# Down projections fed with operand sums from DRAM, in a two-layer decoder trunk on one core

## The chip, the core and the metric

The kernel runs on one core of a Trainium2 chip. Its engines work side by side, each through its own list of instructions: PE (TensorE, matrix products), DVE (VectorE), ACT (ScalarE), POOL (GpSimd) and SP (SyncE, which here issues the DMA transfers). They wait for each other through semaphores. The metric is the device time of one execution in microseconds (us); smaller is better. The clock of PE has two levels, 1.2 and 2.4 GHz; the profile gives the granted clock as a share of the higher one.

## The reference

The program is a decoder trunk of two layers over one sequence of 1024 tokens with 1024 features, all in float32. Each layer is a token mixer (HGRN2 in layer 0, a Griffin recurrent block in layer 1) and a SwiGLU feed-forward block of 2816 hidden features, each behind an RMSNorm and with a residual add. Only the feed-forward blocks and the residual stream are touched here:

```python
def swiglu(h, w_in, w_out):
    gate, up = jnp.split(h @ w_in, [D_FF], axis=-1)
    return (jax.nn.silu(gate) * up) @ w_out

for l in range(DEPTH):
    hn = rmsnorm(x, norm_mix[l])
    mix = hgrn2_mixer(hn, ...) if l % N_MIXERS == 0 else rglru_mixer(hn, ...)
    x = x + mix
    x = x + swiglu(rmsnorm(x, norm_ffn[l]), ffn_w_in[l], ffn_w_out[l])
return rmsnorm(x, norm_final)
```

## The kernel before

**Number format.** Every float32 operand of a large product is split in two float32r tiles, hi and lo: ACT copies the value into hi (`act(hi[:], src, AF.Copy)`), and DVE or POOL subtracts (lo = value − hi). A product of two such operands is three matmuls, hi·hi, hi·lo and lo·hi, recorded at L263, L264 and L265. Tiles are 128 partitions by 512 elements ([P, H]); instructions issued through a helper that records their order all carry line 93.

**Gate and up.** The feed-forward input product runs over 22 tiles f of 128 hidden features. Each tile takes seven quarter products (Winograd's form of Strassen's algorithm), 84 matmuls in all. The weight quarters a11, a12, a21, a22 (tiles `raw_fi`) come from DRAM; `sums` (L983 to L986) makes the left-hand factors s1 to s4 on POOL; ACT and DVE split them. The products gather in PSUM banks pa, pb, pc, pd; DVE and ACT turn these into the two halves of the hidden tile (c11 and u2 or c22), and `store` (L990) writes them to DRAM (`hd`). The tensor engine's order is the program's order.

**Down.** The output product uses the same seven products again, now over 11 pairs j of hidden tiles. It runs in four rounds r over the 11 pairs (`seq`, 44 steps). In rounds 0, 1 and 2 a step feeds two accumulators, pa and pb, of four PSUM banks each, with 24 matmuls; in round 3 only pa, with 12. So a layer has 3×11×24 + 11×12 = 924 matmuls here. At the end of a round `close_a` and `close_b` add the banks to the residual stream `xT` on DVE (`add_x`), before the next round may overwrite them.

**Operands of down, before.** `loads` (L1078 and on) brings parts of `w_out` (`raw_a`) and halves of the hidden tiles (`ht`) from DRAM: 4, 5, 4 and 1 transfers of 256 KB per step in rounds 0 to 3. `items` (L1091 to L1115) makes the factors from them. In round 1 that is two adds on POOL (L1102, L1103; tiles `ds`), three adds on DVE (`ht`, `dt`) and four lo parts on DVE; in round 2 three adds on POOL (L1111 to L1113), one add and four lo parts on DVE; in round 0 two lo parts on DVE and two on POOL; in round 3 one each. `ahead(n + 1, 1)` at each step makes the factors of the next step and issues the loads of the one after it.

**Residual stream, before.** `xT` is 8 tiles of 128 features by 1024 tokens that stay in SBUF for the whole program (L149).

**What sets the order.** Instructions issued through `ordered` or `keep` run in program order on their engine; the others (the adds of `sums`, `store`, the splits on POOL) are placed by the scheduler of the framework. Buffers are handed out by tag (`BUFS`): a tile of a tag waits until an earlier tile of the tag has been read for the last time.

Of the kernel before, what the change touches and what calls it, by code (L numbers as in the profile page):

```python
# [47 lines left out]
def tile_trunk(  # L48
# [56 lines left out]
    BUFS = {"slab": 57, "raw": 6, "whi": 6, "wlo": 6, "F": 1}  # L105
# [80 lines left out]
    def split(name, src, tag="slab", lo_engine=None, kept=False):  # L186
        """src, [P, H] in float32, as the sum of two float32r tiles."""
# [8 lines left out]
    def halves(name, src, lo_engine=None):  # L196
        """As split, with the low part left to a later call; in program order."""
# [13 lines left out]
    def w_cols(name, w, c0, tag="w", lo_engine=None):  # L211
        """Weights of 128 output features: per k-tile (hi, lo)."""
# [8 lines left out]
    def w_row(name, w, r, lo_engine=None, tag="w"):  # L221
        """Weights of 128 input features: per output tile (hi, lo)."""
# [7 lines left out]
    # The tensor engine's order is the program's. Its stream of large products drives side jobs, generators  # L230
    # that yield how much of the stream to let pass before their next step.
# [64 lines left out]
    def row_scale(name, rs, n_bc):  # L296
        """The rows' factors rs, tokens on partitions, along the free axis of all partitions."""
# [1097 lines left out]
```

## Time and profile before

| what | value |
|---|---|
| time, three runs | 2388.19, 2383.64, 2386.39 us (median 2386.39) |
| profiled execution: its span | 2383.3 us, 3.1 us under that median |
| PE busy | 2265.4 us, 95% of the span |
| DVE busy | 1545.5 us, 65% |
| ACT busy | 915.7 us, 38% |
| POOL busy | 833.9 us, 35% |
| transfers, mean | 83 GB/s |

The span is the time from the first to the last record of the profiled execution; nothing else is known of that execution's own time, so sums are made against the span. The stages follow one another: HGRN2 to about 650 us, the first feed-forward block to about 1337 us (its down projection starts at 1098 us), the recurrent block to about 1690 us, and the second feed-forward block (its down projection starts at 2129 us). Shares of the whole span are means over stages with different limits, so each stage has to be read by itself.

### The profile page before, as it was taken

What the parts mean: (1) busy time and instruction counts of PE and PEld (TensorE: products, weight loads), DVE (VectorE), ACT (ScalarE), POOL (GpSimd) and SP (SyncE); (2) the same over time, 40 slices, a digit from 0 to 9 for tenths busy, and PEclk for the clock granted to TensorE, in tenths of its full rate; (3) what the DMA queues carried; (4) which work ended last, traced back from release to release, by engine and by line L of the source; (5) the groups of instructions that cost most, each with busy time, mean ns of one, the idle gap of its engine ahead of it and who ended that gap; (6) DMA issues with size and microseconds to landing.
All of it is one profiled execution on the core that took longest, in us unless ns stands there. A gap on an engine that the chain in (4) does not pass through costs nothing. (4 is left out here: it accounts for less than half of the span.)

```text
span 2383.3 us, 30347 instructions
## 1 busy us (share of the span) xinstructions
PE 2265.4 (95%) x11022; PEld 1892.7 (79%) x11022; DVE 1545.5 (65%) x2578; ACT 915.7 (38%) x1527; POOL 833.9 (35%) x594
## 2 busy tenths in 40 slices
PE   7999999999979999999989899998799999999898
PEld 6898898888758888887768777877678888877777
DVE  6676657647895444445988767668874444448895
ACT  5222121221343333334334465566343333343345
POOL 5102012020353232333576343223543333235672
PEclk9999999999989999999989999999899999999999
DMA  5001101110112222226454211111122222236452
GB/s 143 27 28 45 36 27 41 32 45 19 32 36 89 89 89 84 81 75 228 156 172 137 63 38 55 50 36 36 40 77 88 88 81 84 84 130 224 159 171 93
DMA packets 216568, 197.08 MB, mean 83 GB/s; under 512 B 12009, under 2 KB 159586, under 8 KB 216418
## 3 DMA queue, kind: packets, MB, share of 16 engines
q1 hardware_dynamic: 216418, 195.15, 25.9%
q8 instruction: 86, 1.41, 0.2%
q14 instruction: 64, 0.52, 0.1%
HBM read 167.83 MB, written 27.26 MB: 82 GB/s over the span
## 5 line engine op out<-in xcount | busy, mean ns | idle before, releaser
L983 POOL TENSOR_TENSOR s<-raw_fi,raw_fi 128x512 f32<-128x512 f32 x44 | 60.4, 1372 | 403.2 <-DMA raw_fi<-in_ffn_w_in_dram 383.1
L93 DVE TENSOR_TENSOR lo_x<-ht,hi_x 128x512 fp32r<-128x512 f32 x132 | 143.0, 1111 | 41.0 <-ACT hi_x L93 25.0
L263 PE MATMUL pa<-hi_x,hi_w 128*128 128x512 f32 (+1 forms) x364 | 146.3, 402 | 23.4 <-ACT hi_x L93 15.7
L93 DVE TENSOR_TENSOR lo_s<-s,hi_s 128x512 fp32r<-128x512 f32 x88 | 66.9, 760 | 147.5 <-ACT hi_s L93 147.5
L93 ACT ACTIVATE hi_a<-raw_fi 128x512 fp32r<-128x512 f32 x132 | 83.3, 632 | 194.5 <-PE pc L264 79.1
L265 PE MATMUL pa<-hi_x,lo_w 128*128 128x512 f32 (+1 forms) x364 | 144.9, 398 | 9.4 <-DVE lo_w L93 9.4
L264 PE MATMUL pa<-lo_x,hi_w 128*128 128x512 f32 (+1 forms) x364 | 144.9, 398 | 3.5 <-DVE lo_x L93 3.5
L264 PE MATMUL pa<-lo_t_n,hi_s 128*128 128x512 f32 x336 | 133.4, 397 | 11.5 <-DVE lo_t_n L201 11.5
L191 POOL TENSOR_TENSOR lo_w<-raw_a,hi_w 128x512 fp32r<-128x512 f32 x66 | 91.4, 1392 | 135.1 <-ACT hi_w L93 126.3
L93 DVE TENSOR_TENSOR lo_a<-raw_fi,hi_a 128x512 fp32r<-128x512 f32 x128 | 90.5, 708 | 68.5 <-ACT hi_a L93 68.4
L265 PE MATMUL pa<-hi_t_n,lo_s 128*128 128x512 f32 x336 | 132.9, 395 | 0.0
L263 PE MATMUL pa<-hi_t_n,hi_s 128*128 128x512 f32 x336 | 132.4, 394 | 0.0
L93 ACT ACTIVATE hi_s<-s 128x512 fp32r<-128x512 f32 x88 | 55.6, 632 | 152.1 <-PE pa L264 85.4
L263 PE MATMUL pb<-hi_x,hi_w 128*128 128x512 f32 x264 | 105.0, 398 | 3.8 <-DVE xT L93 3.8
L263 PEld LDWEIGHTS pa<-hi_x,hi_w 128*128 128x128 f32 x364 | 71.7, 197 | 41.6 <-ACT hi_x L93 17.7
L265 PE MATMUL pb<-hi_x,lo_w 128*128 128x512 f32 x264 | 104.4, 395 | 0.0
L264 PE MATMUL pb<-lo_x,hi_w 128*128 128x512 f32 x264 | 104.3, 395 | 0.0
L459 PEld LDWEIGHTS lv<-qp,k 128*128 128x128 f32 x768 | 98.7, 191 | 6.6 <-PE pg L265 0.5
L93 ACT ACTIVATE hi_s<-raw_fi 128x512 fp32r<-128x512 f32 x88 | 55.4, 632 | 126.1 <-PE pd L264 61.0
L93 DVE TENSOR_TENSOR lo_w<-ds,hi_w 128x512 fp32r<-128x512 f32 x88 | 92.1, 1054 | 10.7 <-ACT hi_w L93 10.5
L93 ACT ACTIVATE hi_w<-ds 128x512 fp32r<-128x512 f32 x88 | 54.9, 626 | 110.4 <-PE pb L264 29.4
L459 PE MATMUL lv<-qp,k 128*128 128x64 f32 x768 | 96.3, 267 | 0.1
(357 smaller groups left out, 7053.2 us busy)
## 6 DMA issues: line engine op xcount, KB each, us to landing
raw_a<-in_ffn_w_out_dram SPq DMA_DIRECT2D x220, 256.0 KB, 3.2
raw_fi<-in_ffn_w_in_dram SPq DMA_DIRECT2D x180, 256.0 KB, 3.0
ht<-hd SPq DMA_DIRECT2D x88, 256.0 KB, 5.3
hd<-c SPq DMA_DIRECT2D x48, 256.0 KB, 2.1
hd<-u SPq DMA_DIRECT2D x40, 256.0 KB, 3.0
xr<-in_x_dram SPq DMA_DIRECT2D x16, 256.0 KB, 5.5
raw_v<-in_hgrn_w_in_dram SPq DMA_DIRECT2D x16, 256.0 KB, 3.0
raw_f<-in_hgrn_w_in_dram SPq DMA_DIRECT2D x16, 256.0 KB, 2.8
```

The lines of the kernel that those rows point to most:

```text
L93: ins = f(*args, **kwargs)
L191: ins = (lo_engine.tensor_tensor if lo_engine else tt)(lo[:], src, hi[:], ALU.subtract)
L263: pe(mm(pt, wh, xh, start=st[0], stop=False, skip_group_check=skip))
L264: pe(mm(pt, wh, xl, start=False, stop=False, skip_group_check=skip))
L265: pe(mm(pt, wl, xh, start=False, stop=st[1], skip_group_check=skip))
L459: mm(lvc(c).rearrange("p (b m) -> p b m", m=m), ct(kt, c), second(ct(qp, c)), start=True, stop=True,)
L983: add(s1, a21, a22, ALU.add)
```

## The change

**Sums made early.** In the gate/up loop POOL now also makes the operand sums of the down projection, once per pair j: `x_sums` (four subtractions of hidden halves: t1, t3, t2, t4) and `w_sums` (four loads of `w_out` parts at L1039, then four adds: s1, s3, s2, s4). Each result, and three of the four hidden halves, is written to DRAM by `spill` (L1009). A layer has 44 + 44 such adds.

**Down loads finished operands.** `loads` brings 4 tiles per step in rounds 0 to 2 and 2 in round 3 (14 per pair in both versions); no sum is left in the down projection. `items` only splits: three lo parts on DVE and one on POOL per step of rounds 0 to 2 (all four on DVE before step 4). The splits are made two steps ahead and loads three (`ahead(n + 2, 3)`); those of steps 0 and 1 stand at the end of the gate/up loop, and their hi and lo tiles of the weights use the tags whi and wlo; later ones use slab.

**Residual stream.** `xT` becomes 16 tiles of [P, H] under a tag x with 16 buffers. After the norm ahead of the feed-forward block has read a tile, `put_away` writes it to DRAM; `bring_back` loads 4, 8 and 4 of them ahead of the loads of steps (0, 6), (1, 6) and (3, 4). In between the tag's buffers hold c11, u2, c22 and the tiles of `w_sums` (`da`). The transfers added per layer are 11 × 11 + 32 = 153 of 256 KB.

The core of the diff (removed comments and the parts that follow from it left out):

```diff
-    BUFS = {"slab": 57, "raw": 6, "whi": 6, "wlo": 6, "F": 1}
+    BUFS = {"slab": 57, "x": 16, "raw": 6, "whi": 6, "wlo": 6, "F": 1}
...
-    xT = [cp.tile([P, S], F32, name=f"xT{d}") for d in range(KT)]
+    xT = {}
+    xd = {(d, half): dp.tile([P, H], F32, name=f"xd{d}_{half}") for half in range(NHALF) for d in range(KT)}
...
+    def put_away(d, half):
+        nc.sync.dma_start(xd[d, half][:], half_of(d, half))
+        del xT[d, half]
+
+    def bring_back(ds, half):
+        for d in ds:
+            keep(nc.sync.dma_start(half_of(d, half), xd[d, half][:]))
...
+        def x_sums(j):
+            b12, b11, b22, b21 = [hidden.pop((f, half))[:] for f in (2 * j, 2 * j + 1) for half in range(2)]
+            add(b11, b12, b11, ALU.subtract)
+            spill(hd["t1"][j], b11)
+            add(b12, b22, b12, ALU.subtract)
+            spill(hd["t3"][j], b12)
+            add(b22, b22, b11, ALU.subtract)
+            spill(hd["t2"][j], b22)
+            add(b21, b21, b22, ALU.subtract)
+            spill(hd["t4"][j], b21)
...
+            add(a22, a21, a22, ALU.add)
+            spill(wd["s1"][j], a22)
...
-            s1, s2 = t2k("D", f"ds1{nm}"), t2k("E", f"ds2{nm}")
-            if r == 1:
-                b11, b21, b12, b22 = ht[top, 1][:], ht[bot, 1][:], ld[3], ld[4]
-                keep(add(s1[:], a21, a22, plus))
-                keep(add(s2[:], s1[:], a11, sub))
-                t2 = t2k("A", f"dt2{nm}")
-                tt(b11, b12, b11, sub)
-                tt(t2[:], b22, b11, sub)
-                tt(b21, b21, t2[:], sub)
-                return pair(f"6{nm}", s2[:], t2[:]), pair(f"5{nm}", s1[:], b11)
...
+            keys = (("s2", "t2"), ("s1", "t1")) if r == 1 else (("s3", "t3"), ("s4", "b22"))
+            return [fetch(f"{k}{nm}", d[k][j][:], t) for ks in keys for k, d, t in zip(ks, (wd, hd), ("raw", "slab"))]
...
+            tag = "w" if r == 0 and j < 2 else "slab"
+            first = pair(f"1{nm}", ld[0], ld[1], None if n < 4 else nc.gpsimd, tag)
+            return first, pair(f"2{nm}", ld[2], ld[3], None, tag) if len(ld) > 2 else None
...
+        backs = {(0, 6): [(0, 1)], (1, 6): [(0, 0), (DG, 0)], (3, 4): [(DG, 1)]}
...
-            ahead(n + 1, 1)
-            for m in (2, 3) if r == 3 else ():
+            ahead(n + 2, 3)
+            if n == 5:
+                sums_due()
+            for m in (3, 4, 5) if r == 3 else ():
```

POOL in the gate/up loop of layer 0, around tiles f = 12 and 13. Before it has four sums per tile (`s1`, `s2`, then the two that overwrite `raw_fi`):

```order
L983 TENSOR_TENSOR s1_0_12_8013<-raw_fi0_12_1_0_8009,raw_fi0_12_1_1_8011 128x512
L984 TENSOR_TENSOR s2_0_12_8014<-s1_0_12_8013,raw_fi0_12_0_0_7968 128x512
L986 TENSOR_TENSOR raw_fi0_12_0_0_7968<-raw_fi0_12_0_0_7968,raw_fi0_12_1_0_8009 128x512
L985 TENSOR_TENSOR raw_fi0_12_0_1_7970<-raw_fi0_12_0_1_7970,s2_0_12_8014 128x512
L983 TENSOR_TENSOR s1_0_13_8160<-raw_fi0_13_1_0_8156,raw_fi0_13_1_1_8158 128x512
L984 TENSOR_TENSOR s2_0_13_8161<-s1_0_13_8160,raw_fi0_13_0_0_8115 128x512
L986 TENSOR_TENSOR raw_fi0_13_0_0_8115<-raw_fi0_13_0_0_8115,raw_fi0_13_1_0_8156 128x512
L985 TENSOR_TENSOR raw_fi0_13_0_1_8117<-raw_fi0_13_0_1_8117,s2_0_13_8161 128x512
```

The sums of one tile are followed by those of the next. The same place of the changed kernel, with `da` the parts of `w_out` and `c11`, `u2` the hidden halves of tiles 10 and 11:

```order
L1000 TENSOR_TENSOR s1_0_12_8298<-raw_fi0_12_1_0_8294,raw_fi0_12_1_1_8296 128x512
L1001 TENSOR_TENSOR s2_0_12_8299<-s1_0_12_8298,raw_fi0_12_0_0_8253 128x512
L1023 TENSOR_TENSOR u2_0_10_8013<-c11_0_10_7935,u2_0_10_8013 128x512
L1003 TENSOR_TENSOR raw_fi0_12_0_0_8253<-raw_fi0_12_0_0_8253,raw_fi0_12_1_0_8294 128x512
L1041 TENSOR_TENSOR da0_6_11_8165<-da0_6_10_8163,da0_6_11_8165 128x512
L1043 TENSOR_TENSOR da0_6_10_8163<-da0_6_00_8159,da0_6_10_8163 128x512
L1045 TENSOR_TENSOR da0_6_00_8159<-da0_6_11_8165,da0_6_00_8159 128x512
L1002 TENSOR_TENSOR raw_fi0_12_0_1_8255<-raw_fi0_12_0_1_8255,s2_0_12_8299 128x512
L1047 TENSOR_TENSOR da0_6_01_8161<-da0_6_01_8161,da0_6_00_8159 128x512
L1025 TENSOR_TENSOR c11_0_10_7935<-c11_0_11_8089,c11_0_10_7935 128x512
L1000 TENSOR_TENSOR s1_0_13_8452<-raw_fi0_13_1_0_8448,raw_fi0_13_1_1_8450 128x512
L1001 TENSOR_TENSOR s2_0_13_8453<-s1_0_13_8452,raw_fi0_13_0_0_8407 128x512
```

Between the sums of tile 12 and those of tile 13 six adds now stand on POOL (t1, four of `w_sums`, t3); two more (t2, t4) follow `s2` of tile 13.

SP's list for the same tiles, before: one weight quarter after another, with the two hidden halves of a tile between them.

```order
L990 DMA hd0_10_6015<-c11_0_10_7673 128x512
L93 DMA raw_fi0_13_0_0_8115<-in_ffn_w_in_dram 128x4x128
L990 DMA hd0_10_6015<-u2_0_10_7743 128x512
L93 DMA raw_fi0_13_0_1_8117<-in_ffn_w_in_dram 128x4x128
L93 DMA raw_fi0_13_1_0_8156<-in_ffn_w_in_dram 128x4x128
L93 DMA raw_fi0_13_1_1_8158<-in_ffn_w_in_dram 128x4x128
L990 DMA hd0_11_6016<-c11_0_11_7820 128x512
L93 DMA raw_fi0_14_0_0_8262<-in_ffn_w_in_dram 128x4x128
```

No transfer in it reads what POOL writes. And the list of the changed kernel (`da` loads, `ht1d`, `hb11d`, `ws1d` to `ws4d` the spills):

```order
L1039 DMA da0_6_00_8159<-in_ffn_w_out_dram 128x512
L1039 DMA da0_6_01_8161<-in_ffn_w_out_dram 128x512
L1039 DMA da0_6_10_8163<-in_ffn_w_out_dram 128x512
L1039 DMA da0_6_11_8165<-in_ffn_w_out_dram 128x512
L1009 DMA ht1d0_5_6075<-u2_0_10_8013 128x512
L93 DMA raw_fi0_13_0_1_8409<-in_ffn_w_in_dram 128x4x128
L93 DMA raw_fi0_13_1_0_8448<-in_ffn_w_in_dram 128x4x128
L1009 DMA ws1d0_6_6120<-da0_6_11_8165 128x512
L1009 DMA ws3d0_6_6142<-da0_6_10_8163 128x512
L1009 DMA ws2d0_6_6131<-da0_6_00_8159 128x512
L1009 DMA ws4d0_6_6153<-da0_6_01_8161 128x512
L93 DMA raw_fi0_13_1_1_8450<-in_ffn_w_in_dram 128x4x128
```

The last weight quarter of tile 13 (`raw_fi0_13_1_1`), which `s1` of tile 13 reads, stands behind the four spills of `w_sums`, and these wait for the adds at L1041 to L1047, which stand on POOL behind `s2` of tile 12.

DVE in round 1 of the down projection of layer 0, before: the factors of step (1, 4), from the first sum on, with one sum of step (1, 5) between them.

```order
L93 TENSOR_TENSOR dt20_1_4_10201<-ht0_9_0_10137,ht0_8_1_9563 128x512
L93 TENSOR_TENSOR ht0_8_0_10135<-ht0_9_0_10137,ht0_8_0_10135 128x512
L93 TENSOR_TENSOR ht0_9_1_9567<-ht0_9_1_9567,dt20_1_4_10201 128x512
L93 TENSOR_TENSOR lo_w60_1_4_10206<-ds20_1_4_10198,hi_w60_1_4_10205 128x512
L93 TENSOR_TENSOR lo_x60_1_4_10210<-dt20_1_4_10201,hi_x60_1_4_10209 128x512
L93 TENSOR_TENSOR ht0_10_1_9611<-ht0_10_0_10193,ht0_10_1_9611 128x512
L93 TENSOR_TENSOR lo_x50_1_4_10218<-ht0_8_1_9563,hi_x50_1_4_10217 128x512
L93 TENSOR_TENSOR lo_w50_1_4_10214<-ds10_1_4_10197,hi_w50_1_4_10213 128x512
```

Three sums and four lo parts make one step. The changed kernel, lo parts of steps (1, 3) to (1, 5), where `ld_` tiles are the operands loaded:

```order
L93 TENSOR_TENSOR lo_x20_1_3_10502<-ld_t10_1_3_10359,hi_x20_1_3_10501 128x512
L93 TENSOR_TENSOR lo_x10_1_4_10558<-ld_t20_1_4_10403,hi_x10_1_4_10557 128x512
L93 TENSOR_TENSOR lo_w20_1_4_10562<-ld_s10_1_4_10405,hi_w20_1_4_10561 128x512
L93 TENSOR_TENSOR lo_x20_1_4_10566<-ld_t10_1_4_10407,hi_x20_1_4_10565 128x512
L93 TENSOR_TENSOR lo_x10_1_5_10606<-ld_t20_1_5_10455,hi_x10_1_5_10605 128x512
L93 TENSOR_TENSOR lo_w20_1_5_10610<-ld_s10_1_5_10457,hi_w20_1_5_10609 128x512
L93 TENSOR_TENSOR lo_x20_1_5_10614<-ld_t10_1_5_10459,hi_x20_1_5_10613 128x512
```

Per step seven instructions have become three, and the sums have left the engine.

## Rows read from the trace of the kernel before

**Rows 1.** Page, part 1: busy time, share of span, instructions
```profile
PE 2265.4 (95%) x11022; PEld 1892.7 (79%) x11022; DVE 1545.5 (65%) x2578; ACT 915.7 (38%) x1527; POOL 833.9 (35%) x594
```

**Rows 2.** Windows: gate/up loop, start and middle of a down projection
```profile
core 0: us, PE busy (x) PEld busy (x) DVE busy (x) ACT busy (x) POOL busy (x), PEclk, DMA share, GB/s
750.00:1000.00 250.00, 250.00 (x1104) 207.01 (x1103) 112.19 (x171) 94.08 (x158) 74.28 (x52) 1.00 0.27 83
1120.00:1130.00 10.00, 10.00 (x46) 8.29 (x45) 5.47 (x5) 4.86 (x9) 4.29 (x5) 1.00 1.04 386
1170.00:1290.00 120.00, 108.03 (x439) 86.88 (x439) 112.03 (x124) 46.39 (x82) 84.49 (x46) 0.93 0.52 169
```

**Rows 3.** Groups by line, PE, first down projection: busy | idle, releasers
```profile
L263 PE MATMUL pa<-hi_x,hi_w 128*128 128x512 f32 x139 | 57.1, 410 | 10.9 <-ACT hi_x L93 7.0 <-ACT hi_w L93 3.9
L264 PE MATMUL pa<-lo_x,hi_w 128*128 128x512 f32 x138 | 56.6, 410 | 1.4 <-DVE lo_x L93 1.4
L265 PE MATMUL pa<-hi_x,lo_w 128*128 128x512 f32 x138 | 56.5, 410 | 4.4 <-DVE lo_w L93 4.4
L263 PE MATMUL pb<-hi_x,hi_w 128*128 128x512 f32 x132 | 52.7, 399 | 1.8 <-DVE xT L93 1.8
```

**Rows 4.** The same view of the second down projection
```profile
L263 PE MATMUL pa<-hi_x,hi_w 128*128 128x512 f32 x139 | 56.6, 407 | 9.7 <-ACT hi_x L93 5.8 <-ACT hi_w L93 3.9
L264 PE MATMUL pa<-lo_x,hi_w 128*128 128x512 f32 x138 | 55.7, 404 | 1.3 <-DVE lo_x L93 1.3
L265 PE MATMUL pa<-hi_x,lo_w 128*128 128x512 f32 x138 | 55.7, 404 | 4.9 <-DVE lo_w L93 4.9
L263 PE MATMUL pb<-hi_x,hi_w 128*128 128x512 f32 x132 | 52.3, 396 | 2.0 <-DVE xT L93 2.0
```

**Rows 5.** Windows of both down projections; columns as in rows 2
```profile
1110.00:1120.00 10.00, 8.65 (x31) 7.06 (x32) 8.31 (x6) 5.41 (x10) 8.17 (x6) 0.83 1.01 369
1160.00:1170.00 10.00, 7.74 (x33) 5.82 (x32) 9.70 (x12) 2.83 (x5) 5.02 (x4) 1.00 0.69 242
1170.00:1180.00 10.00, 8.20 (x29) 6.29 (x29) 10.00 (x16) 2.82 (x5) 3.25 (x4) 0.83 0.65 220
1220.00:1250.00 30.00, 21.82 (x71) 16.93 (x70) 26.30 (x28) 12.33 (x22) 24.43 (x15) 0.77 0.55 169
2200.00:2210.00 10.00, 8.22 (x30) 6.26 (x29) 10.00 (x15) 3.20 (x6) 5.13 (x4) 0.83 0.59 197
2250.00:2280.00 30.00, 22.94 (x78) 18.29 (x79) 26.30 (x29) 13.24 (x24) 24.00 (x14) 0.77 0.54 175
```

**Rows 6.** Groups by line, DVE, first down projection
```profile
L93 DVE TENSOR_TENSOR lo_w<-ds,hi_w 128x512 fp32r<-128x512 f32 x44 | 46.1, 1054 | 5.3 <-ACT hi_w L93 5.2
```

**Rows 7.** Groups by line, POOL, first down projection
```profile
L1102 POOL TENSOR_TENSOR ds<-raw_a,raw_a 128x512 f32<-128x512 f32 x11 | 27.6, 2507 | 26.6 <-DVE lo_w L93 21.8 <-DMA ht<-hd 4.8
```

**Rows 8.** Timeline, DVE beside POOL: start, duration, instruction
```profile
685.50 0.68 DVE L93 TENSOR_TENSOR hs_n<-hs_n,hs_n 128x512 f32<-128x512 f32 x1
686.10 1.75 DVE L93 TENSOR_TENSOR lo_s<-s,hi_s 128x512 fp32r<-128x512 f32 x1
```

**Rows 9.** Timeline of POOL at that place
```profile
685.66 1.64 POOL L983 TENSOR_TENSOR s<-raw_fi,raw_fi 128x512 f32<-128x512 f32 x1 [10.06 <-DVE lo_s L93]
```

**Rows 10.** Groups by line, POOL, gate/up loop
```profile
L984 POOL TENSOR_TENSOR s<-s,raw_fi 128x512 f32<-128x512 f32 x17 | 29.5, 1733 | 1.3
L985 POOL TENSOR_TENSOR raw_fi<-raw_fi,s 128x512 f32<-128x512 f32 x17 | 22.0, 1292 | 20.4 <-DVE lo_a L93 20.4
```

**Rows 11.** Timeline, DVE, end of a gate/up tile
```profile
864.97 0.69 DVE L93 TENSOR_TENSOR lo_s<-s,hi_s 128x512 fp32r<-128x512 f32 x1 [2.01 <-ACT hi_s L93]
865.58 0.68 DVE L93 TENSOR_TENSOR c<-u,pc 128x512 f32<-128x512 f32 x1
```

**Rows 12.** Timeline, PE, the product that follows
```profile
866.99 0.39 PE L263 MATMUL pc<-hi_n,hi_s 128*128 128x512 f32 x1
```

**Rows 13.** Page, part 6: DMA issues, KB each, us to landing
```profile
ht<-hd SPq DMA_DIRECT2D x88, 256.0 KB, 5.3
```

More of the change, by code (lines that the diff above doesn't have):

```diff
@@ L340, in normed @@
                 keep(ins)
+            put_away(d, half)
             return h
@@ L943, in ffn @@
         K2 = KT // 2
-        hd = [dp.tile([P, S], F32, name=f"hd{l}_{f}") for f in range(NF)]
         add = nc.gpsimd.tensor_tensor
+        spilled = lambda n: [dp.tile([P, H], F32, name=f"{n}d{l}_{j}") for j in range(NF // 2)]
+        hd = {k: spilled(f"h{k}") for k in ("b11", "b21", "b22", "t1", "t2", "t3", "t4")}
+        wd = {k: spilled(f"w{k}") for k in ("s1", "s2", "s3", "s4")}
         def products(pts, name, srcs, op, first=True, w_lo=None):
@@ L1052, in ffn, with fetch, pair @@
         sub, plus = ALU.subtract, ALU.add
[L1053 to L1066 removed]
+        def fetch(name, src, tag="slab"):
+            t = t2k(tag, f"ld_{name}")
+            keep(nc.sync.dma_start(t[:], src))
+            return t[:]
+        def w_part(name, f, cols, tag="raw"):
+            return fetch(name, w_out[f * P : (f + 1) * P, cols * H : (cols + 1) * H], tag)
+        def pair(name, wsrc, xsrc, w_lo, tag):
+            w = split(f"w{name}", wsrc, tag, w_lo)
             return w, split(f"x{name}", xsrc)
@@ L1128, in ffn @@
         lds, its = {}, {}
+        backs = {(0, 6): [(0, 1)], (1, 6): [(0, 0), (DG, 0)], (3, 4): [(DG, 1)]}
         def ahead(n, n_ld):
-            for m in range(n_ld + 1):
-                if n + m < len(seq) and n + m not in lds:
-                    lds[n + m] = loads(*seq[n + m])
-            if n < len(seq) and n not in its:
-                its[n] = items(*seq[n], lds[n])
+            if n in lds and n not in its:
+                its[n] = items(n, *seq[n], lds[n])
+            for m in range(n + 1, min(n + n_ld + 1, len(seq))):
+                if m not in lds:
+                    for d, half in backs.get(seq[m], ()):
+                        bring_back(range(d, d + DG), half)
+                    lds[m] = loads(*seq[m])
         WLO = [nc.gpsimd if c == "1" else None for c in WL]
@@ L1144, in ffn @@
             rest(f, quarter(f, 0, 0), quarter(f, 0, 1), *begun[f][2:])
+        made = []
         for f in range(2 + NBT, NF - 1):
+            if f % 2 or f in (4, 8):
+                later.append((w_sums, len(made)))
+                made.append(f)
             rest(f, *begin(f))
@@ L1149, in ffn @@
             lds[n] = loads(*seq[n])
-        rest(NF - 1, *b0)
+        rest(NF - 1, *b0, lambda: lds.update({2: loads(*seq[2])}))
+        for n in range(2):
+            its[n] = items(n, *seq[n], lds[n])
         sops.clear()
@@ L1231, in final @@
                 for j in range(4):
-                    pe(nc.tensor.transpose(pt[:, j * P : (j + 1) * P], xT[4 * g + j][:, t0 : t0 + P], ident[:]))
+                    xs = half_of(4 * g + j, half)[:, (c0 + i) * P : (c0 + i + 1) * P]
+                    pe(nc.tensor.transpose(pt[:, j * P : (j + 1) * P], xs, ident[:]))
                 ot = slab(f"ot{nm}_{i}_{g}")
```

81 lines of the change are left out of this document (43 added, 38 removed).

## The prediction

> **What bounds the kernel now.** I read the page's busy shares first [rows 1]: PE is busy 95% of the span, so at most 118 us (2383.3 − 2265.4) are idle, and a busy PE is not always a fast one. So I went by stage, with the windows [rows 2]. In the gate/up loop PE is busy 250.00 of 250 us at clock 1.00, with 1104 matmuls, 0.2264 us each; a tile of 84 takes 19.0 us. DVE is busy 45% and POOL 30% there, and PE waits for nobody. In the middle of a down projection it is the reverse: DVE is busy 112 of 120 us, PE 108, and the clock's mean is 0.93. A step of 24 matmuls would take 24 × 0.2264 = 5.43 us there.
>
> Then the groups by line of PE in both down projections, for what ended its waits. In the first it waits for ACT's hi parts (7.0 + 3.9), for DVE's lo parts (1.4 + 4.4) and for the adds into xT (1.8), together 18.5 us [rows 3]; in the second 5.8 + 3.9 + 1.3 + 4.9 + 2.0 = 17.9 us [rows 4]. ACT is named most, though its hi parts are short; they come late because the sums that they read do.
>
> Why the sums are late: a DVE instruction with two SBUF inputs takes 0.68 us alone and 1.75 us when one of POOL (1.64 us) has started just before it [rows 8, 9]; in down the mean of a lo part is 1054 ns [rows 6], and POOL's first sum takes 2507 ns [rows 7], where 1292 is the shorter mean of the gate/up loop [rows 10]. So the two take turns. A turn of DVE costs 0.61 us (start to start of two neighbours, 865.58 − 864.97) [rows 11], one of POOL 1.3. A step of round 1 has seven on DVE and two on POOL, 4.3 + 2.6 = 6.9 us; of round 2, five and three, 3.1 + 3.9 = 7.0 us; both are above 5.43. Round 0, with two and two, needs 3.8. Over 22 steps that makes 22 × 1.5 = 33 us of backlog per layer, of which the operands made ahead can absorb some. In the trace 28 us are lost per layer, as the next paragraph adds up.
>
> The clock's part comes from the windows in which it fell to its lower level [rows 5]. PE at 1.2 GHz does half the work, so a window loses (1 − PEclk) of its length if PE has work: 1.7 + 1.7 + 0.23 × 30 = 10.3 us in the first down projection, 1.7 + 6.9 = 8.6 in the second. Removable in all: 18.5 + 17.9 + 10.3 + 8.6 = 55.3 us.
>
> The Trainium skill states, in "SBUF — State Buffer", section "Who interferes with whom", that a VectorE instruction with two SBUF inputs and a GpSimd one that reads SBUF exclude each other, whichever starts first, for the whole instruction. By that rule the turns above add up, as the trace agrees with its 1.75 against 0.68 us; it also speaks against this change, since what leaves one stage is put in turns with DVE in another. Were the two to share the port instead, POOL's new adds would cost DVE nothing and the third term below would be 0.
>
> **The change part by part.** *Down.* A step of rounds 0 to 2 keeps three lo parts on DVE and one on POOL: 3 × 0.61 + 1.3 = 3.1 us of turns against 5.43. ACT's four hi parts are no more than before. So the backlog goes, and with it the waits and the falls of the clock: −55.3 us. What is late next is the load of the operands. There are four transfers per step. Eight can be under way, and one lands in 5.3 us [rows 13], so two steps' worth lands where one is asked for. In bytes it is 4 × 0.262 MB in 5.43 us, 193 GB/s, and the start of a down projection already ran at 386 with PE full [rows 2]. I take 0; its bound is a rival.
>
> *Adds into xT.* The 1.8 and 2.0 us arise because seven DVE instructions stand between the adds of pa and those of pb; four lo parts do now. They may go, or stay with the falls at 1170 and 2200 (1.7 each): 0 to 7.2 us, and I keep 1, since four turns (2.4 us) fit in the 2.7 us that the 12 matmuls of pb take.
>
> *Gate/up.* POOL gets 88 adds per layer: a pair of tiles has 16 instead of 8. PE is full there, so nothing can be gained. Three things could be lost. First, PE's operands: s1 and s2 of the next tile are made some 13 us before PE needs them, so a later sum is hidden as long as POOL keeps pace. POOL's pace is 16 × 1.3 = 21 us alone or 16 × 1.73 = 28 us in turns with DVE (the longer mean [rows 10]), of 38.0 per pair. Second, the loop through SP: `a22` of the next tile now waits behind the spills of w_sums, so POOL waits for a landing once or twice a pair, 3 to 5 us each. That gives 28 + 5 = 33, at worst 38, which is just the period. Third, DVE's own lateness: the add that reads pc ends at 866.26 and PE goes on adding to pc at 866.99 [rows 11, 12], 0.73 us later. A lo part stretched by 1.07 us just ahead of that add stalls PE by 0.34 us. It can happen in the 11 tiles of a layer with ten POOL instructions, 22 in all: 0 to 7.5 us. I take 4, half of them.
>
> *Junction.* The splits of the first three down steps stand ahead of the last tile's closing work on ACT and DVE (nine lo parts, 5.5 us of DVE turns), partly in slack. The nearest row for a stage that starts with operands not yet there is the fall at 1110 (1.7 us) with its wait. Bounds 0 and 6 us for both layers; I take 2.
>
> *End of round 3 and the transfers of xT.* The adds of the last round now need tiles brought back from DRAM. 32 transfers per layer at 386 GB/s are 22 us of transfer time beside a PE that does not read them; the bring-back stands at least five steps (27 us) ahead of its use. The last steps hand over to the next stage's norm, and its weights' loads stand in the same SP list: 0 to 6 us, and I take 2. The norm ahead of the gate/up loop only gains writes that nobody waits for: 0.
>
> Sum: −55.3 + 1 + 4 + 2 + 2 = −46.3 us. 2383.3 − 46.3 = 2337.0 us as a span. The median of the runs shown is 3.1 us above the profiled span, which gives 2340 us, 1.9% faster.
>
> **The rivals.**
>
> *Loads stay late* (faster, half the gain). The bring-backs go through the same queue ahead of loads. 16 tiles per layer, 4.2 MB, at 386 GB/s are 10.9 us of queue; if none of it is hidden that is 22 us in both layers, and at the six places where they stand the clock could fall for 1.7 us each, 10 us more. 2340 + 32 = 2372. Against it: loads are issued three steps (16 us) ahead, and the busiest window still had PE at 10.00 of 10 us [rows 2]. A milder form, half of this, gives 2356.
>
> *Each small stall of the gate/up loop pulls the clock down* (no change). 22 stalls of 0.34 us with a fall of 1.7 us each are 45 us instead of 4: 2381. Against it: between 1160 and 1170 PE was idle for 2.26 us and the clock stayed at 1.00; the falls stand behind longer or repeated waits [rows 5].
>
> *POOL becomes the bound of the gate/up loop* (slower). The place is the loop from POOL's add through the spill in SP's list to the next `a22`, its landing and `s1`. It decides once a pair takes over 38 us: with 8 us of landings, at a mean POOL instruction of 1.87 us. Each 0.1 us above that costs 16 × 0.1 × 20 pairs = 32 us, so the gain is eaten at 2.0 us. At 2.5, POOL's mean for its first sum in the crowded down stage [rows 7], a pair would take 48 us, 200 us more in all; halfway, at 2.2, it is 43, which makes 2340 + 104 = 2444. Against it: 2507 ns were measured with DVE busy over 90%; in gate/up it is at 45% and POOL's longer mean is 1.73 [rows 2, 10]. For it: ten in a row have never run there.
>
> *The change does not do what it says*, because ACT and not DVE is the bound in down: ACT is busy 46 of 120 us [rows 2], so this falls, and I give it no chance of its own.
>
> **How the numbers follow.** The forecast has 0.63, with its own range from all removed and nothing kept (2383.3 − 55.3 + 3.1 = 2331) to every kept term at its upper end (7.2 + 7.5 + 6 + 6 = 26.7: 2358). Late loads have 0.20 (2352 to 2375), the clock's fall 0.08 (2370 to 2386), POOL as the bound 0.09, of which two thirds end slower than before. The range of 2330 to 2372 holds the forecast and most of the late loads. Faster by over 0.2% (4.8 us, about what a measurement tells apart here): 0.63 + 0.20 + 0.03 of the clock's fall = 0.86; within it 0.06; slower 0.08.
>
> **What would show each step.** In the changed profile's windows of down, PE should be busy over 99% at clock 1.00 and DVE near 45 to 55%; a wait there that ends with a DMA speaks for late loads. In the gate/up loop, PE busy should stay above 98%, POOL go from 30% to 60 to 75%, and its adds stay under 1.8 us. A PE wait for ACT's hi part of s1 or s2 there is POOL as the bound. Falls of PEclk outside the down projections would show the second rival. The forecast is wrong if the gate/up loop's 19.0 us per tile grows by more than 0.5 us, or if a down step takes more than 5.6 us.

## The result and the profile after

The changed kernel takes 2333.28 us (median of 4 runs, 2326.74 to 2338.94) against 2387.29 before: a ratio of 0.9773, interval 0.9754 to 0.9793, or 54 us less. The forecast was 2340 us. The profiled execution has a span of 2325.0 us, 58.3 less than that of before. It belongs to the fastest of the four runs (2326.74 us), so the stages below add up to some 4 us more than the medians differ by.

The page of the changed kernel, part 1 and the clock of part 2:

```profile
PE 2248.9 (97%) x11022; PEld 1880.9 (81%) x11022; DVE 1474.5 (63%) x2476; ACT 924.1 (40%) x1527; POOL 907.1 (39%) x674
PEclk9999999999999999999999999999999999999999
```

PE is busy 97% of a shorter span, and POOL has gone from 834 to 907 us [rows 1]. By stage, with the windows that answer to [rows 2] and the middle of the second down projection as the last row:

```profile
core 0: us, PE busy (x) PEld busy (x) DVE busy (x) ACT busy (x) POOL busy (x), PEclk, DMA share, GB/s
750.00:1000.00 250.00, 249.54 (x1096) 204.78 (x1095) 142.32 (x170) 92.96 (x157) 157.94 (x111) 1.00 0.53 173
1115.00:1125.00 10.00, 10.00 (x46) 8.28 (x45) 7.25 (x10) 8.59 (x15) 4.76 (x4) 1.00 1.06 392
1165.00:1285.00 120.00, 120.00 (x531) 99.38 (x530) 58.96 (x77) 54.47 (x94) 40.13 (x31) 1.00 0.63 205
2165.00:2285.00 120.00, 120.00 (x531) 99.38 (x530) 60.06 (x80) 54.28 (x93) 32.84 (x25) 1.00 0.58 191
```

In the middle of both down projections PE is busy 120.00 of 120 us at clock 1.00, with 531 matmuls where 439 were done in the first of them before; DVE has fallen there from 112 to 59 us. In the gate/up loop POOL has doubled, DVE is stretched from 112 to 142 us, and PE is idle for 0.46 of 250 us, with 8 matmuls fewer (8 × 0.2264 = 1.8 us behind). PE by line in the first three rounds of the first down projection, for [rows 3]:

```profile
L276 PE MATMUL pa<-hi_x,hi_w 128*128 128x512 f32 x148 | 57.6, 389 | 0.0
L277 PE MATMUL pa<-lo_x,hi_w 128*128 128x512 f32 x147 | 57.2, 389 | 0.0
L278 PE MATMUL pa<-hi_x,lo_w 128*128 128x512 f32 x147 | 57.2, 389 | 0.0
L276 PE MATMUL pb<-hi_x,hi_w 128*128 128x512 f32 x132 | 51.3, 389 | 0.0
```

Not one of the waits is left, the adds into xT included, and a matmul takes 389 ns in place of 410 because the clock no longer falls there.

PE's matmuls come in the same order in both kernels, so the time between two given matmuls can be compared (us, start to start). The borders are fixed matmul numbers: 3840, 4320, 8040 and 8400 lie near the edges of the stages named and not on them, the others are the first matmuls of the down projections and of their rounds. A round of 264 matmuls takes 59.8 us when PE never waits. PE takes up a step's second accumulator (pb) only after the next step's first (pa), so each row of a round ends with the first product of the next round.

| stage | before | after | difference |
|---|---|---|---|
| HGRN2 | 629.3 | 627.4 | −1.9 |
| start of the first feed-forward block | 133.8 | 130.7 | −3.1 |
| gate/up loop, layer 0 | 332.3 | 334.4 | +2.1 |
| down, layer 0: round 0 | 69.1 | 59.8 | −9.3 |
| round 1 | 80.3 | 59.8 | −20.5 |
| round 2 | 60.2 | 59.8 | −0.4 |
| round 3 and the recurrent block | 359.2 | 357.8 | −1.5 |
| start of the second feed-forward block | 106.8 | 107.0 | +0.2 |
| gate/up loop, layer 1 | 355.0 | 358.5 | +3.5 |
| down, layer 1: round 0 | 66.0 | 59.8 | −6.2 |
| round 1 | 80.6 | 59.8 | −20.8 |
| round 2 | 60.4 | 59.8 | −0.6 |
| round 3 to the end | 40.9 | 40.9 | 0.0 |

The rounds gave 57.8 us, 41 of them in round 1, the gate/up loops took back 5.6. What round 0 lost before lies at two places: 6.5 us (layer 0) and 3.3 us (layer 1) in its first three steps, and 2.8 us in each layer at its end, at the first product of round 1. In the first layer (PE, before):

```profile
1109.49 0.50 PE L263 MATMUL pa<-hi_x,hi_w 128*128 128x512 f32 x1 [2.86 <-ACT hi_x L93]
1164.21 0.47 PE L263 MATMUL pa<-hi_x,hi_w 128*128 128x512 f32 x1 [2.26 <-ACT hi_w L93]
```

### The profile page after: what moved, and what is told of

Its sections match the earlier page's. It is cut to its first block, busy times and chain, and to the rows that moved or that the text cites. A ratio compares the mean times of both kernels' runs of the same rounds, so it can differ in the third digit from the quotient of the medians.

```text
span 2325.0 us, 30979 instructions
## 1 busy us (share of the span) xinstructions
PE 2248.9 (97%) x11022; PEld 1880.9 (81%) x11022; DVE 1474.5 (63%) x2476; ACT 924.1 (40%) x1527; POOL 907.1 (39%) x674
## 5 line engine op out<-in xcount | busy, mean ns | idle before, releaser
L93 DVE TENSOR_TENSOR lo_s<-s,hi_s 128x512 fp32r<-128x512 f32 x88 | 95.3, 1083 | 118.2 <-ACT hi_s L93 118.2
L93 DVE TENSOR_TENSOR lo_a<-raw_fi,hi_a 128x512 fp32r<-128x512 f32 x128 | 125.7, 982 | 57.5 <-ACT hi_a L93 55.7
L276 PE MATMUL pa<-hi_x,hi_w 128*128 128x512 f32 (+1 forms) x364 | 140.4, 386 | 0.0
L278 PE MATMUL pa<-hi_x,lo_w 128*128 128x512 f32 (+1 forms) x364 | 139.8, 384 | 0.0
L277 PE MATMUL pa<-lo_x,hi_w 128*128 128x512 f32 (+1 forms) x364 | 139.6, 384 | 0.0
L93 DVE TENSOR_TENSOR lo_x<-ld_t,hi_x 128x512 fp32r<-128x512 f32 x88 | 76.3, 873 | 94.3 <-ACT hi_x L93 65.6
L204 POOL TENSOR_TENSOR lo_w<-ld_s,hi_w 128x512 fp32r<-128x512 f32 x44 | 60.1, 1366 | 158.7 <-ACT hi_w L93 118.4
L204 POOL TENSOR_TENSOR lo_f<-raw_f,hi_f 128x512 fp32r<-128x512 f32 x14 | 18.3, 1312 | 191.4 <-ACT hi_f L93 191.4
L93 DVE TENSOR_TENSOR lo_s<-raw_fi,hi_s 128x512 fp32r<-128x512 f32 x84 | 71.9, 857 | 33.0 <-ACT hi_s L93 32.8
L204 POOL TENSOR_TENSOR lo_w<-ld_a,hi_w 128x512 fp32r<-128x512 f32 x36 | 48.5, 1347 | 98.3 <-ACT hi_w L93 84.2
```

The lines of the kernel that those rows point to most:

```text
L204: ins = (lo_engine.tensor_tensor if lo_engine else tt)(lo[:], src, hi[:], ALU.subtract)
L276: pe(mm(pt, wh, xh, start=st[0], stop=False, skip_group_check=skip))
L277: pe(mm(pt, wh, xl, start=False, stop=False, skip_group_check=skip))
L278: pe(mm(pt, wl, xh, start=False, stop=st[1], skip_group_check=skip))
```

## The experiments

**Was it the sums, or the deeper lookahead?** One kernel takes the lookahead away from the changed kernel, one gives it to the kernel before.

```diff
-            ahead(n + 2, 3)
+            ahead(n + 1, 1)
...
```

> The changed kernel with the splits made one step ahead and the loads two, as before the change, instead of two and three; the sums stay in the gate/up loop. Theory of turns: nothing is lost inside a round, where 3.1 us of turns stand against 5.43; at the three round borders of a layer, where DVE's adds into xT wait for PE with less prepared behind them, up to 2.5 us each: 2333 to 2348 us. Rival, the lookahead made the gain: most of the 54 us come back, 2370 to 2387.

2338.1 us, ratio 0.9800 (0.9784 to 0.9815). All rounds 0 to 2 stay at 59.8 us; round 3 with the recurrent block after it takes 360.9 us in place of 357.8, and the last round 46.7 in place of 40.9.

```diff
-            ahead(n + 1, 1)
+            ahead(n + 2, 2)
...
```

> The kernel before with nothing but the deeper lookahead: factors made two steps ahead and loads one more. The sums stay in the down projection. Theory of turns: rounds 1 and 2 still need 6.9 and 7.0 us per step against 5.43, so the backlog stays and only a step's worth of lead is won per layer: 2375 to 2390 us (tiles for the hidden halves can even hold the loads up). Rival, the lookahead made the gain: 2333 to 2345.

2393.66 us, ratio 1.0029 (1.0018 to 1.0040), 4 us above the range expected. Round 1 still takes 75.3 and 76.3 us, and round 0 grew to 74.9 and 73.2. The lookahead alone gains nothing.

**Which engine's sums?** Two kernels put one kind of sum back into the changed kernel's down projection. First those of the hidden halves, on DVE:

```diff
+            if r == 1:
+                w2, b12, w1, b11, b22, b21 = ld
+                tt(b11, b12, b11, sub)
+                tt(b22, b22, b11, sub)
+                tt(b21, b21, b22, sub)
+                keep(nc.sync.dma_start(hd["t4"][j][:], b21))
...
```

> The changed kernel with the sums of the hidden halves put back into the down projection, on DVE (three per step of round 1, one in round 2; six transfers per step in round 1, and t4 written to DRAM from there); the sums of w_out stay in the gate/up loop. Theory of turns (DVE and POOL exclude each other, and the sum of their turns is the limit): round 1 needs 6 x 0.61 + 1.3 = 5.0 us per step, round 2 4 x 0.61 + 1.3 = 3.7, both under the 5.43 of PE, so the down projections stay full and the gate/up loop has 12 instead of 16 POOL adds per pair: 2328 to 2340 us. Rival, DVE's own instructions were the limit before: six instead of seven per step give most of the loss back, 2365 to 2380. Rival, the lookahead made the gain: as the changed kernel, 2333.

2359.76 us, ratio 0.9890 (0.9866 to 0.9913): between what the theories gave, so neither held. Rounds 1 take 76.4 and 76.5 us. They wait for something else, as SP's waits in the first of them show (what was waited for, total us, times, longest):

```profile
SPq L1119 <- DVE lo_w L93: 33.1, 9, 5.5
```

SP's transfers in that round (start, time to issue), and DVE beside them:

```profile
1180.62 0.32 SPq L1119 DMA_DIRECT2D ld_b<-hb12d  x1
1185.22 0.32 SPq L1119 DMA_DIRECT2D ld_s<-ws1d  x1
1185.59 0.43 SPq L1119 DMA_DIRECT2D ld_b<-hb11d  x1
```

```profile
1184.52 0.68 DVE L93 TENSOR_TENSOR lo_w<-ld_s,hi_w 128x512 fp32r<-128x512 f32 x1
...
1188.60 0.69 DVE L93 TENSOR_TENSOR ld_b<-ld_b,ld_b 128x512 f32<-128x512 f32 x1 [2.19 <-DMA ld_b<-hb11d]
1189.21 0.68 DVE L93 TENSOR_TENSOR lo_x<-ld_b,hi_x 128x512 fp32r<-128x512 f32 x1
```

SP holds a weight load (1185.22) back until a lo part on DVE (1184.52) has freed its buffer, and the load of a hidden half stands behind it (1185.59). Three instructions after that lo part DVE stops ahead of the sum that reads this half (1188.60). In DVE's list the sums of step 7 stand ahead of the lo parts of step 5 (the framework's scheduler put them there: once `fix` is off, L725, `ordered` fixes no order), so the next lo part waits for a load which waited for the one before: a circle of one step per landing, 7 us (from 1185.22 the held-back load comes again at 1192.38). If that is so, it should break when SP issues the halves first:

> x_sums_in_down with one thing changed: per step SP issues the loads of the hidden halves before those of the weight sums, so they no longer stand behind a load that waits for a lo part on DVE. x_sums_in_down lost 16.6 us in each round 1; its DVE list has the sums of step 7 ahead of the lo parts of step 5, and the load that these sums read stood behind one that waits for the lo part of step 4. If that circle was the cause, round 1 falls from 76.4 to 60 to 64 us and the total to 2330 to 2340; if six DVE instructions or seven transfers per step are too many, 2355 to 2362.

2330.04 us, ratio 0.9759 (0.9738 to 0.9781), with rounds 1 of 60.5 and 63.6 us at the same number of instructions and transfers. DVE's pattern of sums and lo parts in the middle of the round is the same in both. The order of SP's loads was the cause. So DVE may keep its sums; it is enough that POOL's have left. The 3.8 us that round 1 of layer 1 still loses have no cause shown.

Now the sums of `w_out`, back on POOL in the down projection:

```diff
+                if r == 1:
+                    keep(add(s1[:], a21, a22, plus))
+                    keep(add(s2[:], s1[:], a11, sub))
...
+                else:
+                    keep(add(s1[:], a11, a21, sub))
+                    keep(add(s2[:], a22, s1[:], sub))
+                    keep(add(s2[:], ld[3], s2[:], sub))
```

> The changed kernel with the sums of w_out put back into the down projection, on POOL (two per step of round 1, three in round 2, all four lo parts on DVE there); the sums of the hidden halves stay in the gate/up loop. Theory of turns: round 1 needs 4 x 0.61 + 2 x 1.3 = 5.0 us per step, just under 5.43; round 2 needs 2.4 + 3.9 = 6.3, which is 0.9 too many over 11 steps, 10 us per layer less what two steps of lead absorb, with falls of the clock on top: 2340 to 2358 us. Rival, DVE alone was the limit: four DVE instructions per step are few, 2328 to 2335. Rival, the lookahead made the gain: 2333.

2338.41 us, ratio 0.9802 (0.9782 to 0.9822), 1.6 us below the theory's range. Round 1 takes 59.8 us in both layers, round 2 takes 64.2; the round that should suffer is the one that does. The total says less, since the gate/up loops gave back 5.6 us here.

**The same question asked of the kernel before.** Each engine's sums left out, and nothing else:

> The kernel before without POOL's sums of w_out in rounds 1 and 2 of the down projection (left out of the computation: the loaded tiles a11, a21, a22 stand in their place; every transfer, DVE's sums and all lo parts stay). In the trace of before round 1 takes 80.3 and 80.6 us instead of 59.8. Theory of turns: round 1 has 7 x 0.61 = 4.3 us of DVE left and nothing to take turns with, so both rounds 1 fall to 60 to 63 us: 2344 to 2356 us. Rival, the five transfers per step or DVE's order hold round 1 up, as the order did in x_sums_in_down: round 1 stays above 75 us, 2375 to 2388.

> The kernel before without DVE's sums of the hidden halves in rounds 1 and 2 (left out of the computation: the loaded halves stand in their place; every transfer, POOL's sums and all lo parts stay). Theory of turns: round 1 needs 4 x 0.61 + 2 x 1.3 = 5.0 us per step, under 5.43: both rounds 1 fall to 60 to 65 us, 2345 to 2360 us; either engine's sums taken alone free the round. Rival, POOL's sums by themselves are too slow or too late (chain add, add, hi, lo through two buffers): round 1 stays above 72 us, 2370 to 2388.

2337.08 us, ratio 0.9787 (0.9773 to 0.9802), and 2338.09 us, ratio 0.9792 (0.9777 to 0.9807), both 7 us below the ranges expected. Rounds 1 fall from 80 to 59.8 us in both, in both layers, and so does the wait at the end of round 0 (2.8 us per layer, to 0.0), which the ranges had not counted: it too was a wait for round 1's sums. The windows of before's rounds 1 and 2, and of round 1 without POOL's and without DVE's sums (columns as in rows 2):

```profile
1167.00:1247.00 80.00, 68.03 (x266) 54.07 (x265) 72.03 (x90) 27.00 (x48) 54.49 (x27) 0.90 0.52 165
1248.00:1308.00 60.00, 60.00 (x265) 49.44 (x264) 51.09 (x48) 23.29 (x42) 41.52 (x27) 1.00 0.45 145
```

```profile
1162.00:1222.00 60.00, 60.00 (x266) 49.70 (x265) 53.21 (x89) 26.06 (x46) 0.00 (x0) 1.00 0.75 242
```

```profile
1163.00:1223.00 60.00, 60.00 (x266) 49.70 (x265) 50.40 (x54) 27.11 (x48) 39.72 (x26) 1.00 0.71 234
```

In the second of these kernels POOL still works 40 of 60 us, and in the first DVE 53; neither slows PE. Only the two together do, which a limit of either engine by itself does not explain. Without POOL, 89 DVE instructions take 53.2 us, 0.60 each; before, 90 took 72.0.

**What one turn costs.** POOL and DVE of the kernel before, in round 2, where DVE never waits and POOL hardly (start, duration):

```profile
1259.42 1.79 DVE L93 TENSOR_TENSOR lo_w<-ds,hi_w 128x512 fp32r<-128x512 f32 x1
1261.13 1.78 DVE L93 TENSOR_TENSOR lo_x<-ht,hi_x 128x512 fp32r<-128x512 f32 x1
1262.83 1.78 DVE L93 TENSOR_TENSOR lo_w<-ds,hi_w 128x512 fp32r<-128x512 f32 x1
1264.53 0.68 DVE L93 TENSOR_TENSOR lo_x<-ht,hi_x 128x512 fp32r<-128x512 f32 x1
1265.13 1.78 DVE L93 TENSOR_TENSOR lo_w<-ds,hi_w 128x512 fp32r<-128x512 f32 x1
```

```profile
1260.73 1.62 POOL L1113 TENSOR_TENSOR ds<-raw_a,ds 128x512 f32<-128x512 f32 x1
1262.32 1.74 POOL L1111 TENSOR_TENSOR ds<-raw_a,raw_a 128x512 f32<-128x512 f32 x1
1264.74 1.62 POOL L1112 TENSOR_TENSOR ds<-raw_a,ds 128x512 f32<-128x512 f32 x1 [0.68 <-POOL ds L1111]
```

DVE goes from one start to the next in 1.70 us when a POOL add gets in between, and in 0.60 (1264.53 to 1265.13) when none does. A POOL turn therefore costs 1.1 us, not the 1.3 of its own duration. (The Trainium skill, in "SBUF — State Buffer", section "Who interferes with whom", calls what the two contend for an exclusive lock; the turns agree, with 0.2 us less than POOL's 1.3 of whole duration.) The windows above count what the two engines did there, so they test this price: 90 × 0.60 + 27 × 1.1 = 84 us were done in 80 of round 1, 48 × 0.60 + 27 × 1.1 = 58.5 in 60 of round 2, and 54 × 0.60 + 26 × 1.1 = 61 in 60 of round 1 without DVE's sums. In round 2 of w_sums_in_down 52 and 32, 66 us, were done in 64:

```profile
1221.00:1285.00 64.00, 62.32 (x265) 48.56 (x264) 62.78 (x52) 26.91 (x48) 51.53 (x32) 1.00 0.73 248
```

What a round asks for is another count. At these prices a step of round 1 (seven on DVE, two on POOL) asks for 6.4 us and one of round 2 (five and three) for 6.3, against PE's 5.43. Round 2 lost next to nothing all the same because part of its work was done in round 1: all its sums on DVE, and on POOL four of the eleven sets of three adds, as L1111, the first add of each set, shows (round 2 starts at 1247.60):

```profile
1226.99 4.68 POOL L1111 TENSOR_TENSOR ds<-raw_a,raw_a 128x512 f32<-128x512 f32 x1 [4.24 <-DVE lo_w L93]
...
1244.05 1.74 POOL L1111 TENSOR_TENSOR ds<-raw_a,raw_a 128x512 f32<-128x512 f32 x1
```

So the 20 us lost in round 1 are the overload of both rounds.

**What made round 0 faster?**

```diff
-                tags = ("x", "x") if j < 2 else ("raw", "raw") if j < 3 else ("raw", "slab")
+                tags = ("slab", "slab") if j < 3 else ("raw", "slab")
...
```

> The changed kernel with the loads of the first three steps of down in the tag slab, as before, whose tiles come free at the end of the gate/up loop, and the third step's loads not issued ahead of the last tile. In the traces round 0 takes 69.1 and 66.0 us before and 59.8 after. If the early loads made that part of the gain, both rounds 0 go back to 65 to 70 us and the total to 2343 to 2350; if the missing sums made it, 2331 to 2337.

2345.19 us, ratio 0.9812 (0.9787 to 0.9838). The total lies in the first theory's range, the rounds do not: in the trace rounds 0 take 61.2 and 63.2 us, so waits come back, but 1.4 and 3.4 us, in the first two steps, where before lost 6.5 and 3.3; the gate/up loop of layer 0 also took 337.4 us, 3 more. The median is 10.5 us above the profiled run (2334.70) and isn't explained by these stages. PE at the start of its second down projection:

```profile
L276 PE MATMUL pa<-hi_x,hi_w 128*128 128x512 f32 x48 | 19.5, 407 | 2.0 <-ACT hi_x L93 2.0
L277 PE MATMUL pa<-lo_x,hi_w 128*128 128x512 f32 x47 | 18.9, 403 | 1.4 <-DVE lo_x L93 1.4
```

Leaving out POOL's sums, on the other hand, still leaves 66.1 and 63.2 us in rounds 0: it frees the end of the round and not its start. So the early loads are a part of the gain at the start. The deeper lookahead is not the rest (one_step_ahead kept 59.8 us); the splits made at the end of the gate/up loop or POOL's second lo part may be, and were not tried apart.

**Where did the gate/up loop lose 5.6 us?** DVE, POOL and PE of the changed kernel at one of its stalls:

```profile
898.95 1.84 DVE L93 TENSOR_TENSOR lo_s<-s,hi_s 128x512 fp32r<-128x512 f32 x1 [1.11 <-ACT hi_s L93]
900.71 0.67 DVE L93 TENSOR_TENSOR c<-u,pc 128x512 f32<-128x512 f32 x1
```

```profile
897.37 1.62 POOL L1045 TENSOR_TENSOR da<-da,da 128x512 f32<-128x512 f32 x1
898.95 1.29 POOL L1002 TENSOR_TENSOR raw_fi<-raw_fi,s 128x512 f32<-128x512 f32 x1
```

```profile
900.74 0.39 PE L278 MATMUL pd<-hi_t_n,lo_a 128*128 128x512 f32 x1
901.44 0.50 PE L276 MATMUL pc<-hi_n,hi_s 128*128 128x512 f32 x1 [0.31 <-DVE c L93]
```

A lo part that started beside a POOL add takes 1.84 us; the add that reads pc ends at 901.38, and PE's next product in pc starts at 901.44 in place of 900.97. It takes the adds of `w_out` parts to lose it: with them gone from the loops (w_sums_in_down) these take 332.3 and 355.0 us, with the sums of the hidden halves gone instead (x_sums_in_down) 333.7 and 357.3. If the late add is the whole loss, freeing pc earlier gives it back:

```diff
+            c22 = t2k("u", f"c22_{nm}")
+            act(c22[:], pc_[:], AF.Copy)
             product(pa, f"s3_{nm}", s3, "t3", False)
...
-            c22 = t2k("u", f"c22_{nm}")
-            tt(c22[:], u3[:], pc_[:], ALU.add)
+            tt(c22[:], c22[:], pa[:], ALU.add)
```

> The changed kernel with the bank pc freed early in the gate/up loop: ACT copies it into c22's tile when its product is done, and DVE adds pa to that copy, so PE no longer waits there for a DVE add that stands behind a lo part stretched by POOL. In the changed kernel's trace the loop lost 2.1 us in layer 0 and 3.5 in layer 1 against before, in stalls of up to 0.6 us ahead of that product. If the late add is the cause, both loops return to 332.3 and 355.0 us (within 0.7) and the total falls by 4 to 6 us, to 2327 to 2330. Rival, the loop loses its time to late weights or POOL: no change, 2331 to 2336; ACT's 44 more copies could also hold up hi parts: slower, up to 2345.

2327.65 us, ratio 0.9745 (0.9726 to 0.9764). The loops take 332.3 and 355.0 us, to the tenth what they took before, with PE full although POOL does as much as in the changed kernel:

```profile
750.00:1000.00 250.00, 250.00 (x1105) 207.01 (x1104) 141.65 (x173) 100.60 (x171) 160.08 (x113) 1.00 0.54 174
```

> x_sums_halves_first (2330.0 us) with the same early copy of pc: 12 POOL adds per pair in the gate/up loop, the sums of the halves on DVE in the down projection. Its gate/up loops lost 1.3 and 1.2 us, its rounds 1 lose 0.7 and 3.8. If the stalls go here too: 2326 to 2329; rival, no change: 2329 to 2332.

2325.57 us, ratio 0.9745 (0.9720 to 0.9770); its loops take 332.3 and 355.0 us as well. Both versions have medians below the changed kernel's, but their intervals overlap its own, and the two can't be told apart.

**What would POOL as the bound have cost?**

```diff
+            more = t2k("B", f"more{l}_{j}")[:]
+            for _ in range(8):
+                add(more, a11, a22, ALU.add)
```

> The changed kernel with eight more POOL adds per pair (88 more per layer, into a tile that nobody reads), 24 per pair in place of 16: what POOL as the bound would cost, the rival that was forecast as slower. At the mean POOL add of the changed gate/up loop (1.43 us) 24 take 34 us of a pair's 38.0; with landings of 3 to 8 us ahead of s1 that is 37 to 42. Theory that POOL binds once adds and landings pass 38 us: the pairs with these adds grow by 0 to 5 us each, 22 of them, 2335 to 2440, nearest 2380, and PE waits for ACT's hi parts of s1, s2. Rival, the landings are hidden and only the turns with DVE grow: 2333 to 2345.

2452.32 us, ratio 1.0277 (1.0255 to 1.0298), above the range expected. The loops grow by 61.8 and 60.1 us against the changed kernel. POOL is busy 214 of 250 us, and the product in pc waits for the add on DVE:

```profile
800.00:1050.00 250.00, 215.43 (x891) 174.34 (x892) 142.03 (x142) 77.16 (x131) 214.28 (x150) 0.92 0.43 139
```

```profile
L276 PE MATMUL pc<-hi_n,hi_s 128*128 128x512 f32 x68 | 33.9, 498 | 44.3 <-DVE c L93 44.3
```

The loop of layer 0 is 63.9 us longer than before's, and the trace shows two kinds of places (a regular pair of tiles, and tiles 5 and 6; columns as in rows 2):

```profile
958.40:998.40 40.00, 38.71 (x170) 31.41 (x169) 25.06 (x27) 14.19 (x25) 33.26 (x24) 1.00 0.46 147
783.00:840.20 57.20, 42.91 (x169) 34.47 (x168) 26.30 (x26) 14.13 (x25) 50.95 (x36) 0.85 0.42 138
```

The regular pair has its 24 POOL instructions in 40.0 us in place of 38.0; the four such pairs of tiles 12 to 19 take 39.5 to 43.0, within the 0 to 5 us more that were expected of each. But `w_sums` does not stand ahead of every second tile alone: it is called for tiles 3, 4, 5 and 7, 8, 9 in a row. There POOL has 36 instructions in two tiles, and tiles 4 to 6 and 8 to 10 alone lose 46.8 of the 63.9 us. The forecast had left this crowding out. The place where PE felt it was not the one expected (hi parts of s1 and s2) but DVE's late add: lo parts of the next tile, which wait for POOL, stand ahead of it on DVE.

**The residual stream alone.**

> The kernel before with nothing but the residual stream in 16 tiles that leave the chip ahead of the gate/up loop and come back in the down projection, 64 transfers of 256 KB more. Theory: nobody waits for the writes and the reads come early, 2383 to 2390 us, no change. In the changed kernel the stage that starts the first feed-forward block took 3.1 us less than before; if the smaller tiles did that (an add or a norm step waits for half a tile), that stage falls from 133.8 to about 131 us here, 2381 to 2385. Rival, the transfers hold up loads in rounds 0 and 1, where before's operands are late already: 2390 to 2405.

2392.49 us, ratio 1.0021 (1.0011 to 1.0030): above the theory's range and in that of the rival. In the kernel before the round trip costs 6.5 us: round 2 (66.4 and 67.6 us) and round 0 (70.6, 68.6) lose more than round 1 (75.3, 75.2) gains. PE waits for lo parts and, longer than before, for the adds into xT:

```profile
L275 PE MATMUL pa<-lo_x,hi_w 128*128 128x512 f32 x154 | 63.6, 413 | 7.4 <-DVE lo_x L93 7.4
L274 PE MATMUL pb<-hi_x,hi_w 128*128 128x512 f32 x132 | 52.7, 399 | 4.8 <-DVE xT L93 4.8
```

The start of the first block took 137.3 us here, so the smaller tiles alone don't explain the 3.1 us that it gained in the changed kernel.

## Why the prediction was right, and where its numbers were not

**What bounds down.** Right: DVE and POOL exclude each other, and taking either one's sums away frees the rounds. Its arithmetic was wrong in size. It put POOL's turn at 1.3 us, and so a step at 6.9 and 7.0 us and the backlog at 33 us per layer. A turn costs 1.1, which makes 6.4 and 6.3 us and 20 us per layer; the 16 adds into xT, which it left out of the turns, are worth another 9.6. The trace lost 23.6 and 24.1 us per layer that way: 2.8 at the first product of round 1, 20.4 and 20.8 in round 1, 0.4 and 0.5 in round 2.

The other 6.5 and 3.3 us lay in the first three steps of down, whose turns (3.8 us per step) were not too many: there the operands were late. The prediction counted these waits and falls among those that go with the backlog, and listed the place as a cost of the change (the junction, 2 us). That they went as well was luck, as far as its argument goes.

**Removable 55.3 us.** The rounds gave 57.8. Reading the idle rows and the falls of PEclk together gave the right sum before the causes were known apart.

**Terms kept.** Adds into xT: 1 us forecast, none measured. Gate/up: 4 forecast, 5.6 measured, by the mechanism named, a stretched lo part ahead of the add on pc [rows 11, 12]; it came at 12 tiles of the two loops together, with stalls of 0.1 to 0.6 us, where 0.34 was forecast. Junction: 2 forecast, none measured; twelve lo parts of the first three steps stand there on DVE, not nine, and the last ends at 1093.03, 2 us before PE's first product of down (1095.16). End of round 3: 2 forecast; with the recurrent block it is −1.5. Kept terms were 9 in the sum and 4 in the trace. The remaining difference is 5 us gained in HGRN2 and the start of the first block. They have no cause in the change that a run showed: in other kernels here the latter stage took 130 to 138 us with 16 tiles and 134 to 137 with 8, and the profiled execution itself lies 6.5 us under its kernel's median. Against that median the forecast is 7 us too long.

**The rivals.** Late loads: no wait for a transfer is left in the rows above; but x_sums_in_down fell into one, through the order of the lists, not through bandwidth (271 GB/s from 1155 to 1231 us, where 392 were reached). Clock: in both gate/up loops it stayed at 1.00 through stalls of up to 0.6 us. POOL as the bound: it had room, a mean add of 1.4 us, and waits of 75.5 us for weights that it still could afford:

```profile
L1001 POOL TENSOR_TENSOR s<-s,raw_fi 128x512 f32<-128x512 f32 x16 | 26.3, 1643 | 1.3
L1000 POOL TENSOR_TENSOR s<-raw_fi,raw_fi 128x512 f32<-128x512 f32 x16 | 22.6, 1411 | 75.5 <-DMA raw_fi<-in_ffn_w_in_dram 75.5
L1047 POOL TENSOR_TENSOR da<-da,da 128x512 f32<-128x512 f32 x10 | 15.4, 1535 | 0.2
L1041 POOL TENSOR_TENSOR da<-da,da 128x512 f32<-128x512 f32 x10 | 12.9, 1291 | 13.1 <-DMA da<-in_ffn_w_out_dram 13.1
```

With half as many adds again it bound, and then cost more than the change gives. The 8 us of landings per pair were too many: in the regular pair shown POOL is idle for 6.7 us, 3.8 of them one wait for a landing. The mean of 1.87 us at which it would bind was not tested.

## What to carry to other kernels

When two engines share a resource in turns, count both engines' instructions stage by stage, at a price read from starts in a stretch without waits; a stage is late when the sum passes the time that PE needs there, though neither engine alone does. Count what the program asks for and not what ran in the stage's window, since one stage can do the work of the next. Moving one engine's share to a stage with room is enough, and the price shows up at the one instruction there with the least slack, here a bank of PSUM that can be freed earlier. Before an instruction is moved ahead in a list, look what it waits for and what stands behind it: a load that waits for a buffer, freed by an instruction behind the reader of that load, makes a circle that costs a landing per step. And a cost given per pair is a mean: look whether the work is spread as evenly as the mean supposes.

## What was not expected of the hardware

A POOL add between two DVE instructions costs DVE 1.10 us of start-to-start time, though POOL's add lasts 1.29 alone and shows as 1.6 to 1.7 there. The turns are not always one by one: the POOL add at 1226.99 shows 4.68 us, and DVE started five more instructions, 0.60 us apart, while it waited. The order of the loads within a step in SP's list was worth 30 us (2359.8 against 2330.0) with the same instructions on all engines.
